# Single PSUM banks in place of half double banks in a hybrid encoder kernel

## The chip, the cores and the metric

The kernel runs on one core of one Trainium2 chip. The figure of merit is device microseconds of one execution. TensorE (PE) multiplies, VectorE (DVE), ScalarE (ACT) and GpSimd (POOL) do elementwise work, and SyncE (SP) issues the DMA transfers. Matmul results land in PSUM, which has 8 banks; one bank holds 512 float32 values in each of 128 partitions. A tile of 128 x 512 takes one bank, a tile of 128 x 1024 takes two neighbouring banks (a double bank).

## What is computed

Input and output are one sequence of 1024 tokens of width 1024 in float32. There are two layers, each a mixer and a squared-ReLU MLP, all residual with an RMSNorm ahead, and a final RMSNorm:

```python
for layer in range(DEPTH):                     # DEPTH = 2
    if layer % 2 == 0:
        h = rmsnorm(x, e_norm_mix[e])
        x = x + even_mixer(h, ...)             # windowed GQA + pooling mixer
    else:
        h = rmsnorm(x, o_norm_mix[o])
        x = x + odd_mixer(h, ...)              # latent attention + gated recurrence
    x = x + sq_relu_mlp(rmsnorm(x, norm_mlp[layer]), w_mlp1[layer], w_mlp2[layer])
return rmsnorm(x, final_norm)

def sq_relu_mlp(h, w1, w2):
    u = jax.nn.relu(h @ w1)                    # 1024 -> 4096
    return (u * u) @ w2                        # 4096 -> 1024
```

## The kernel before

The program runs through five stages: the even mixer (0 to about 310 us of the trace), the first MLP (to about 957), the odd mixer (to about 1493), the second MLP (to about 2097) and the final norm with the output. Activations are kept transposed, channels on the partitions and tokens on the free axis. A float32 operand is split into a high and a low part in the fast matmul format (L122 makes the high part on ACT, L130 the low part on DVE or POOL), and a product is three matmuls: high x high, high x low, low x high.

**The MLP.** The matrix product is done in 2 x 2 blocks of a seven-product scheme of the Strassen kind. The 4096 hidden channels are 16 pairs of blocks. One product is 12 matmuls of 128 x 512 into one bank of PSUM (L378 in the first matrix product, L498 in the second). A pair uses four banks a, b, c, d and makes seven products in the text's order a, b, c, d, then a, c and d once more: `head` puts the first product in a and copies it out (L396, ACT), `rest` makes the product b and adds it to that copy (L407, DVE), subtracts from c (L410), adds d (L412); then `head2` adds a second product into a, which is read by a ReLU on ACT (L401); c and d get a second product each, read at L419 and L424. The weight blocks are raw blocks or sums of raw blocks (made on POOL), split by L122 and L130 into the tiles `wb`.

**Where the banks come from.** Three pools hold PSUM: `pb` and `pa` with two single banks each, and `p2` with two double banks. In the MLP the pairs take turns (`banks`): the even ones take the four single banks, the odd ones the four halves of the two double banks. Elsewhere `PS` hands out places in turn for projections (`z`, `op`, `o`), sums of squares (`ss`) and broadcasts of the row norms (`rb`): two of `pb`, two of `pa`, and four halves of double banks (`PS2H`). In the attention parts `set_wide` leaves only the four single banks in the rotation, and the double banks hold scores (`s`, `ms`) and gates (`gt`).

**What a tile is.** Waits are made per tile. The two halves of a double bank are one tile, though they lie in two banks: a matmul into one half waits until earlier readers of the other half are done, and the double bank is free for the next user when both halves have been read. A framework orders the instructions of each engine ahead of the run, by operands and by free tiles, so the text's order is not the order on the engine; each engine then works through its own list strictly in turn.

**The norm between stages.** RMSNorm needs a sum over channels: squares are added on POOL or DVE (`square_add`, L245), a matmul with ones gives `ss` (L220), a chain of seven small DVE and ACT instructions makes `rr` (L196 to L211), a matmul against the identity broadcasts it as `rb` (L231), ACT copies it to `RB` (L235), and DVE scales the activations with it (L1528 ahead of an MLP).

Of the kernel before, what the change touches and what calls it, by code (L numbers as in the profile page):

```python
# [9 lines left out]
F32 = mybir.dt.float32  # L10
# [5 lines left out]
P = 128  # L16
S = 1024
# [7 lines left out]
N2 = 512  # L25
# [21 lines left out]
class Trunk:  # L47
    def __init__(self, tc, a, pools, phases):
        self.tc, self.nc, self.a = tc, tc.nc, a
        self.cst, self.gp, self.wp, self.tp, self.sm, self.pb, self.pa, self.p2, self.dr = pools  # L50
        nc = self.nc
        self.uid = 0
        self.cols = self.cst.tile([P, NCOLS], F32, tag="cols", name="cols")
        nc.sync.dma_start(self.cols, a["cols"])
        self.ident = self.cst.tile([P, P], F32, tag="ident", name="ident")
        make_identity(nc, self.ident)
        self.ones = self.cst.tile([P, 1], F32, tag="ones", name="ones")
        nc.vector.memset(self.ones, 1.0)
        self.wide = False
        self.pk = 0  # L60
        self.half = None
        self.halves = {}
        self.wreq = []
        self.wout = []
        for ph in phases:
            self.wreq += self.requests(ph)
# [19 lines left out]
    def PA(self, name):  # L86
        return self.pa.tile([P, N2], F32, tag="a", name=self.nm(name))

    def PS2(self, name):
        return self.p2.tile([P, S], F32, tag="bb", name=self.nm(name))  # L90

    def PS(self, name):

        k = self.pk
        self.pk = (k + 1) % (4 if self.wide else 8)
        return self.PB(name) if k < 2 else self.PA(name) if k < 4 else self.PS2H(name)

    def PS2H(self, name):

        if self.half is None:  # L100
            self.half = self.PS2(name)
            return self.half[:, :N2]
        h, self.half = self.half, None
        return h[:, N2:]

    def set_wide(self, w):
        self.wide = w
        self.pk = 0
        self.half = None

    def pin(self, ins):

# [170 lines left out]

    def banks(self, which):
        if which:
            two = [self.PS2("q"), self.PS2("q")]
            return [x[:, s] for x in two for s in (slice(0, N2), slice(N2, S))]
        return [self.PB("q"), self.PB("q"), self.PA("q"), self.PA("q")]

    def w_stream(self, l, order, second, look=0):  # L290
# [1396 lines left out]
def trunk(tc, a, phases=("even", "mlp0", "odd", "mlp1", "final")):  # L1687
    PSUM = bass.MemoryType.PSUM
    with tc.tile_pool(name="cst", bufs=1) as cst, tc.tile_pool(name="sm", bufs=4) as sm, \
            tc.tile_pool(name="tp", bufs=4) as tp, tc.tile_pool(name="wp", bufs=W_BUFS) as wp, \  # L1690
            tc.tile_pool(name="gp", bufs=G_BUFS) as gp, tc.tile_pool(name="pb", bufs=2, space=PSUM) as pb, \
            tc.tile_pool(name="pa", bufs=2, space=PSUM) as pa, \
            tc.tile_pool(name="p2", bufs=2, space=PSUM) as p2, \
            tc.tile_pool(name="dr", bufs=1, space=bass.MemoryType.DRAM) as dr:
        t = Trunk(tc, a, (cst, gp, wp, tp, sm, pb, pa, p2, dr), phases)
        gains = {"even": "e_norm", "odd": "o_norm", "mlp0": "mlp0", "mlp1": "mlp1"}
        xs = dr.tile([D, S], F32, tag="xs", name="xs")
        xm = [dr.tile([D, S], F32, tag=f"xm{i}", name=f"xm{i}") for i in range(2)]
        box = {}

        def follow(i):

            def make(X):
                ph = phases[i] if i < len(phases) else None
                box[i] = Out(t, X) if ph is None else Final(t, X) if ph == "final" else \
                    Norm(t, X, gains[ph], xs if ph == "odd" else None) if ph in ("even", "odd") else \
                    SNorm(t, X, gains[ph], xm[int(ph[-1])], int(ph[-1]))
                return box[i]
            return make

        X = [t.G("X") for _ in range(NC)]
        first = follow(0)(X)
        for cut in first.cuts:
            for c in range(NC):
                s = slice(*cut)
                tc.nc.sync.dma_start(X[c][:, s], a["x"][c * P:(c + 1) * P, s])
                first.part(c, cut)
        for i, ph in enumerate(phases):
            if ph == "even":
                X = t.even(box[i], follow(i + 1))  # L1720
            elif ph == "odd":
                X = t.odd(box[i], xs, follow(i + 1))
            elif ph != "final":
                t.mlp(int(ph[-1]), box[i], follow(i + 1), f"ut{ph[-1]}_")
# [87 lines left out]
```

## Time and profile before

| what | us |
|---|---|
| median of three runs | 2161.3 |
| the three runs | 2161.3, 2161.65, 2158.78 |
| the profiled execution's own time | 2161.66 |
| its span in the trace | 2159.5 |
| PE busy in the span | 2051.3 (95%) |
| DVE / ACT / POOL busy | 1542.9 / 1065.0 / 823.2 |

Rows of the trace's views read as "start, length, engine, operation out<-in, count"; in square brackets stands how long the engine idled before it and which instruction released it. L378 is line 378 of the kernel before. A matmul's listed length (some 0.39 us) is longer than its share of PE time, since matmuls follow each other in a pipeline. The profiled execution's time is 2.16 us over its span.

### The profile page before, as it was taken

Reading aid. Unit: us, or ns where it says so; the run is one execution under the profiler, and the core shown is the slowest. Engines: PE = TensorE matmul, PEld = TensorE weight load, DVE = VectorE, ACT = ScalarE, POOL = GpSimd, SP = SyncE. Lnnn points to the kernel's source line nnn. Section 1 sums busy time; section 2 is a strip of 40 time slices with the busy share of each in tenths; the row PEclk is TensorE's granted clock in tenths of the full one; section 3 lists DMA queues with packets and bytes.
Section 4 is the critical chain, followed back from the end, with each engine's and each line's share of the span. In section 5 each row is a group of like instructions: output and inputs, shape, how many; then the busy total and the mean of one; then the engine's idle time right before and its main releaser. Section 6 shows DMA issues by size and latency. Waiting matters only on the chain.

```text
span 2159.5 us, 27248 instructions
## 1 busy us (share of the span) xinstructions
PE 2051.3 (95%) x9600; PEld 1688.1 (78%) x9600; DVE 1542.9 (71%) x2365; ACT 1065.0 (49%) x1853; POOL 823.2 (38%) x635
## 2 busy tenths in 40 slices
PE   6989998999999999999997999999899999999997
PEld 5867776787777888888785898888678777788887
DVE  7688868765656877775898888717875655877964
ACT  5236645444544534340565777734645545544423
POOL 4133332332315142242557776463242321522414
PEclk9999999999999999999999999999999999999999
DMA  5630052543448535132102000245443445654302
GB/s 176 144 136 24 11 185 78 176 166 127 151 152 310 176 107 180 55 101 76 35 25 68 11 11 10 79 130 188 135 172 127 152 155 179 236 204 157 127 29 79
DMA packets 115544, 261.32 MB, mean 121 GB/s; under 512 B 19664, under 2 KB 21840, under 8 KB 115408
## 3 DMA queue, kind: packets, MB, share of 16 engines
q1 hardware_dynamic: 115408, 259.59, 35.7%
q8 instruction: 75, 1.23, 0.2%
q14 instruction: 61, 0.50, 0.1%
HBM read 178.28 MB, written 72.35 MB: 116 GB/s over the span
## 4 chain that ended last, share of the span: by engine, by line
PE 72%; DVE 12%; issue 5%; ACT 5%; DMA 3%; POOL 3%; SPq 0%; POOLq 0%; DVEq 0%; ACTq 0%
PE q L498 22%; PE q L378 22%; PE op L185 7%; PE z L185 6%; PE ms L1334 4%; PE o L185 3%; PE cav L1124 2%; PE ctp L1350 2%; DVE th L1443 1%; POOL acc L245 1%; DVE wb L130 1%; DMA X<-xm 1%; DMA raw<-in_e_w_in_dram 1%; PE tp L870 1%; DVE w L1433 0%
## 5 line engine op out<-in xcount | busy, mean ns | idle before, releaser
L378 PE MATMUL q<-hb,wb 128*128 128x512 f32 x2688 | 629.7, 394 | 34.6 <-DVE wb L130 9.8
L378 PEld LDWEIGHTS q<-hb,wb 128*128 128x128 f32 x2688 | 504.1, 189 | 158.2 <-DVE wb L130 12.8
L498 PE MATMUL q<-ub,wb 128*128 128x512 f32 x2352 | 539.3, 391 | 8.8 <-ACT wb L122 7.0
L498 PEld LDWEIGHTS q<-ub,wb 128*128 128x128 f32 x2352 | 443.2, 189 | 104.3 <-ACT wb L122 8.8
L130 DVE TENSOR_TENSOR wb<-raw,wb 128x512 fp32r<-128x512 f32 x268 | 226.6, 851 | 112.6 <-ACT wb L122 112.2
L122 ACT CAST wb<-raw 128x512 fp32r<-128x512 f32 x268 | 164.3, 619 | 183.0 <-PE q L378 112.7
L122 ACT CAST wb<-sum 128x512 fp32r<-128x512 f32 x152 | 93.8, 620 | 183.3 <-PE q L378 100.7
L130 DVE TENSOR_TENSOR ub<-ut,ub 128x512 fp32r<-128x512 f32 x168 | 136.3, 824 | 66.2 <-ACT ub L122 65.8
L122 ACT CAST ub<-ut 128x512 fp32r<-128x512 f32 x168 | 101.4, 618 | 147.2 <-DVE wb L130 18.8
L130 DVE TENSOR_TENSOR wb<-sum,wb 128x512 fp32r<-128x512 f32 x152 | 126.3, 833 | 22.5 <-ACT wb L122 21.5
L185 PE MATMUL z<-Hh,wh 128*128 128x512 f32 x328 | 129.8, 400 | 10.6 <-ACT wh L122 9.6
L245 POOL TENSOR_TENSOR acc<-acc,sq 128x512 f32<-128x512 f32 (+1 forms) x62 | 88.3, 1427 | 123.3 <-ACT sq L244 121.4
L185 PE MATMUL z<-Hl,wh 128*128 128x512 f32 x328 | 130.2, 397 | 4.1 <-DVE Hl L1471 4.0
L185 PE MATMUL z<-Hh,wl 128*128 128x512 f32 x328 | 129.1, 394 | 0.8 <-DVE wl L130 0.8
L323 POOL TENSOR_TENSOR sum<-raw,raw 128x512 f32<-128x512 f32 x28 | 40.3, 1448 | 215.6 <-DMA raw<-in_w_dram 184.4
L332 POOL TENSOR_TENSOR raw<-raw,raw 128x512 f32<-128x512 f32 x32 | 43.5, 1360 | 203.2 <-DVE wb L130 175.6
L1124 PE MATMUL cav<-cpT,VS 128*128 128x256 f32 x512 | 102.7, 305 | 3.6 <-ACT cpT L1353 2.3
L122 ACT CAST wh<-raw 128x1024 fp32r<-128x1024 f32 (+1 forms) x49 | 49.8, 1015 | 111.9 <-PE z L185 39.4
L1334 PE MATMUL ms<-Kt,Qt 128*128 128x512 f32 (+1 forms) x384 | 99.8, 396 | 2.2 <-ACT e L1341 1.4
L185 PE MATMUL op<-yh,wh 128*128 128x512 f32 x252 | 100.0, 398 | 1.4 <-DVE ya L887 0.9
L185 PE MATMUL op<-yl,wh 128*128 128x512 f32 x252 | 98.9, 393 | 0.0
L185 PE MATMUL op<-yh,wl 128*128 128x512 f32 x252 | 98.0, 393 | 0.0
(343 smaller groups left out, 3815.0 us busy)
## 6 DMA issues: line engine op xcount, KB each, us to landing
raw<-in_w_dram SPq DMA_DIRECT2D x140, 512.0 KB, 4.5
xm<-X SPq DMA_DIRECT2D x32, 256.0 KB, 2.0
X<-xm SPq DMA_DIRECT2D x16, 512.0 KB, 6.6
raw<-in_o_w_out_dram SPq DMA_DIRECT2D x16, 512.0 KB, 3.5
raw<-in_o_w_in_dram SPq DMA_DIRECT2D x11, 512.0 KB, 3.5
raw<-in_e_w_in_dram SPq DMA_DIRECT2D x10, 512.0 KB, 5.1
X<-in_x_dram SPq DMA_DIRECT2D x16, 256.0 KB, 5.6
raw<-in_e_w_out_dram SPq DMA_DIRECT2D x8, 512.0 KB, 3.6
```

What stands on the lines that cost most here:

```text
L122: self.nc.scalar.copy(out, x)
L130: e.tensor_tensor(out, x, y, op=ALU.subtract)
L185: self.nc.tensor.matmul(ps, l, r, start=(first and i == 0), stop=(last and i == n - 1))
L245: (eng or nc.gpsimd).tensor_tensor(acc, acc, sq, op=ALU.add)
L323: add(x, blk(p, 1, 0), blk(p, 1, 1), op=ALU.add)
L332: add(x, x, blk(p, 1, 0), op=ALU.add)
L378: nc.tensor.matmul(ps, a, b, start=(first and c == 0 and i == 0), stop=(c == 3 and i == 2), skip_group_check=True)
L498: nc.tensor.matmul(ps[m], a, b, start=(first and j == 0 and i == 0), stop=(j == len(pairs) - 1 and i == 2), skip_group_check=True)
L870: nc.tensor.transpose(tp[:, h * P:(h + 1) * P], pt[h // 2][:, o:o + P], self.ident)
L1124: nc.tensor.matmul(ACC[0][:, (p % 2) * 256:(p % 2 + 1) * 256], VS[h][:, kb * P:(kb + 1) * P], pp[:, t * N2 + ii * 256:t * N2 + (ii + 1) * ...
L1334: nc.tensor.matmul(ps[:, s], l[rows, qs], r[rows, s], start=(i == 0), stop=(i == 2))
L1350: nc.tensor.transpose(tp[:, (2 * i + j) * P:(2 * i + j + 1) * P], pr[j][:, kb * P:(kb + 1) * P], self.ident)
```

## The change

The double-bank pool `p2` stays for scores and gates. A new pool `pc` of four single banks stands beside it, and every product that took a half of a double bank takes a tile of `pc`: in `banks` for the odd pairs of the MLP, and in `PS` for the projections, sums and broadcasts. The pools now name 2 + 2 + 4 + 4 = 12 banks in all; the framework places their tiles in the 8 banks by the time at which each lives. The number of instructions on each engine, the operands and the transfers are the same; the line numbers move up by 7 or 8 (L378 becomes L370, L498 becomes L490, L185 becomes L178, L220 becomes L213, L231 becomes L224).

```diff
--- before.py
+++ after.py
@@ -47,7 +47,7 @@
 class Trunk:
     def __init__(self, tc, a, pools, phases):
         self.tc, self.nc, self.a = tc, tc.nc, a
-        self.cst, self.gp, self.wp, self.tp, self.sm, self.pb, self.pa, self.p2, self.dr = pools
+        self.cst, self.gp, self.wp, self.tp, self.sm, self.pb, self.pa, self.pc, self.p2, self.dr = pools
         nc = self.nc
         self.uid = 0
         self.cols = self.cst.tile([P, NCOLS], F32, tag="cols", name="cols")
@@ -58,7 +58,6 @@
         nc.vector.memset(self.ones, 1.0)
         self.wide = False
         self.pk = 0
-        self.half = None
         self.halves = {}
         self.wreq = []
         self.wout = []
@@ -86,6 +85,9 @@
     def PA(self, name):
         return self.pa.tile([P, N2], F32, tag="a", name=self.nm(name))
 
+    def PC(self, name):
+        return self.pc.tile([P, N2], F32, tag="c", name=self.nm(name))
+
     def PS2(self, name):
         return self.p2.tile([P, S], F32, tag="bb", name=self.nm(name))
 
@@ -93,20 +95,11 @@
 
         k = self.pk
         self.pk = (k + 1) % (4 if self.wide else 8)
-        return self.PB(name) if k < 2 else self.PA(name) if k < 4 else self.PS2H(name)
-
-    def PS2H(self, name):
-
-        if self.half is None:
-            self.half = self.PS2(name)
-            return self.half[:, :N2]
-        h, self.half = self.half, None
-        return h[:, N2:]
+        return self.PB(name) if k < 2 else self.PA(name) if k < 4 else self.PC(name)
 
     def set_wide(self, w):
         self.wide = w
         self.pk = 0
-        self.half = None
 
     def pin(self, ins):
 
@@ -283,8 +276,7 @@
 
     def banks(self, which):
         if which:
-            two = [self.PS2("q"), self.PS2("q")]
-            return [x[:, s] for x in two for s in (slice(0, N2), slice(N2, S))]
+            return [self.PC("q") for _ in range(4)]
         return [self.PB("q"), self.PB("q"), self.PA("q"), self.PA("q")]
 
     def w_stream(self, l, order, second, look=0):
@@ -1690,9 +1682,10 @@
             tc.tile_pool(name="tp", bufs=4) as tp, tc.tile_pool(name="wp", bufs=W_BUFS) as wp, \
             tc.tile_pool(name="gp", bufs=G_BUFS) as gp, tc.tile_pool(name="pb", bufs=2, space=PSUM) as pb, \
             tc.tile_pool(name="pa", bufs=2, space=PSUM) as pa, \
+            tc.tile_pool(name="pc", bufs=4, space=PSUM) as pc, \
             tc.tile_pool(name="p2", bufs=2, space=PSUM) as p2, \
             tc.tile_pool(name="dr", bufs=1, space=bass.MemoryType.DRAM) as dr:
-        t = Trunk(tc, a, (cst, gp, wp, tp, sm, pb, pa, p2, dr), phases)
+        t = Trunk(tc, a, (cst, gp, wp, tp, sm, pb, pa, pc, p2, dr), phases)
         gains = {"even": "e_norm", "odd": "o_norm", "mlp0": "mlp0", "mlp1": "mlp1"}
         xs = dr.tile([D, S], F32, tag="xs", name="xs")
         xm = [dr.tile([D, S], F32, tag=f"xm{i}", name=f"xm{i}") for i in range(2)]
```

The order in which the framework puts the instructions moves with it. Three places on PE follow; `x3` are three matmuls that read alike, and buffer numbers differ between the two programs.

**In the steady first matrix product of an MLP, PE, a pair that took double banks.** Before, `q_4164` holds products a and b, `q_4165` products c and d; the rows are the last of c, then b, then the second product of a, then d:

```order
L378 MATMUL q_4165<-hb_3168,wb_4093 128x512 x3
L378 MATMUL q_4164<-hb_3034,wb_4072 128x512 x3
L378 MATMUL q_4164<-hb_3060,wb_4072 128x512 x3
L378 MATMUL q_4164<-hb_3086,wb_4072 128x512 x3
L378 MATMUL q_4164<-hb_3112,wb_4072 128x512 x3
L378 MATMUL q_4164<-hb_2913,wb_4132 128x512 x3
L378 MATMUL q_4164<-hb_2935,wb_4132 128x512 x3
L378 MATMUL q_4164<-hb_2957,wb_4132 128x512 x3
L378 MATMUL q_4164<-hb_2961,wb_4132 128x512 x3
L378 MATMUL q_4165<-hb_3192,wb_4112 128x512 x3
L378 MATMUL q_4165<-hb_3195,wb_4112 128x512 x3
L378 MATMUL q_4165<-hb_3198,wb_4112 128x512 x3
```

With the change a, b, c, d are `q_4185` to `q_4188`; the rows are the last of b, then c, d and the start of the second product of a:

```order
L370 MATMUL q_4186<-hb_3126,wb_4093 128x512 x3
L370 MATMUL q_4187<-hb_3152,wb_4114 128x512 x3
L370 MATMUL q_4187<-hb_3156,wb_4114 128x512 x3
L370 MATMUL q_4187<-hb_3179,wb_4114 128x512 x3
L370 MATMUL q_4187<-hb_3183,wb_4114 128x512 x3
L370 MATMUL q_4188<-hb_3207,wb_4133 128x512 x3
L370 MATMUL q_4188<-hb_3210,wb_4133 128x512 x3
L370 MATMUL q_4188<-hb_3213,wb_4133 128x512 x3
L370 MATMUL q_4188<-hb_3216,wb_4133 128x512 x3
L370 MATMUL q_4185<-hb_2926,wb_4153 128x512 x3
L370 MATMUL q_4185<-hb_2948,wb_4153 128x512 x3
L370 MATMUL q_4185<-hb_2970,wb_4153 128x512 x3
```

The second product of a stood right behind b, in the same tile; now 24 matmuls of c and d stand between, and a and b are two tiles.

**At the start of the even mixer, PE.** `Hh` and `Hl` are the parts of the loaded input's eight channel blocks, and `z_341` is one double bank that holds a projection in each half, from weights `wh_214` and `wh_220`. Before, behind the last block of the first projection, the whole second one follows:

```order
L185 MATMUL z_276<-Hh_158,wl_221 128x512
L220 MATMUL ss_301<-ones,acc_107 128x1 x4
L185 MATMUL z_341<-Hh_158,wh_214 128x512
L185 MATMUL z_341<-Hl_159,wh_214 128x512
L185 MATMUL z_341<-Hh_158,wl_215 128x512
L185 MATMUL z_341<-Hh_103,wh_220 128x512
L185 MATMUL z_341<-Hl_104,wh_220 128x512
L185 MATMUL z_341<-Hh_103,wl_221 128x512
L185 MATMUL z_341<-Hh_110,wh_220 128x512
```

The 24 matmuls of the second projection (`z_341<-..,wh_220` and its `wl_221`) end with the broadcast `rb_318` one row ahead of the last. With the change the two projections are `z_344` and `z_369`, and both go along with each block as it comes:

```order
L178 MATMUL z_279<-Hl_162,wh_223 128x512
L178 MATMUL z_279<-Hh_161,wl_224 128x512
L213 MATMUL ss_304<-ones,acc_110 128x1 x4
L178 MATMUL z_344<-Hh_161,wh_217 128x512
L178 MATMUL z_369<-Hh_161,wh_223 128x512
L178 MATMUL z_344<-Hl_162,wh_217 128x512
L178 MATMUL z_344<-Hh_161,wl_218 128x512
L178 MATMUL z_369<-Hl_162,wh_223 128x512
L178 MATMUL z_369<-Hh_161,wl_224 128x512
L224 MATMUL rb_321<-ident,rr_319 128x128 x4
L178 MATMUL z_472<-Hh_106,wh_229 128x512
```

The broadcast `rb_321` now follows the last block at once.

**At the start of the first MLP, PE.** The sum and the broadcast of the second half of the tokens. Before:

```order
L378 MATMUL q_3063<-hb_2842,wb_2884 128x512 x3
L378 MATMUL q_3063<-hb_2888,wb_2884 128x512 x3
L378 MATMUL q_3063<-hb_2892,wb_2884 128x512 x3
L220 MATMUL ss_2989<-ones,acc_2758 128x1 x4
L378 MATMUL q_3171<-hb_2838,wb_3037 128x512 x3
L378 MATMUL q_3171<-hb_2842,wb_3037 128x512 x3
L378 MATMUL q_3171<-hb_2888,wb_3037 128x512 x3
L378 MATMUL q_3171<-hb_2892,wb_3037 128x512 x3
L231 MATMUL q_3006<-ident,rr_3004 128x128 x4
L378 MATMUL q_3006<-hb_2913,wb_2966 128x512 x3
```

With the change:

```order
L370 MATMUL q_2977<-hb_2948,wb_2893 128x512 x3
L370 MATMUL q_2977<-hb_2970,wb_2893 128x512 x3
L370 MATMUL q_2977<-hb_2974,wb_2893 128x512 x3
L213 MATMUL ss_3002<-ones,acc_2769 128x1 x4
L370 MATMUL q_3019<-hb_2926,wb_2979 128x512 x3
L370 MATMUL q_3019<-hb_2948,wb_2979 128x512 x3
L370 MATMUL q_3019<-hb_2970,wb_2979 128x512 x3
L370 MATMUL q_3019<-hb_2974,wb_2979 128x512 x3
L224 MATMUL rb_3037<-ident,rr_3017 128x128 x4
L370 MATMUL q_3077<-hb_2850,wb_2896 128x512 x3
```

The broadcast was a half of the tile `q_3006`, and the product `q_3171` with `wb_3037` stood ahead of it; now it has the tile `rb_3037`, and a product with another weight block (`wb_2979`) stands ahead of it. Further up the list the output projections `op` of the even mixer now all stand ahead of the MLP's first product; before, two matmuls of it stood among them.

## The prediction

> **What bounds the kernel now.** I read the page's busy times first, then its chain of work that ended last, then the table by stage, then the list of PE's waits.
>
> ```profile
> span 2159.5 us, 27248 instructions
> PE 2051.3 (95%) x9600; PEld 1688.1 (78%) x9600; DVE 1542.9 (71%) x2365; ACT 1065.0 (49%) x1853; POOL 823.2 (38%) x635
> PE 72%; DVE 12%; issue 5%; ACT 5%; DMA 3%; POOL 3%; SPq 0%; POOLq 0%; DVEq 0%; ACTq 0%
> ```
>
> PE is busy for 2051.3 of 2159.5 us, so whatever a better use of the banks can bring lies within 108 us of PE idling, less what the first loads and the last norm need. No matmul is removed. The next view is busy time by stage; its columns are the window, its length, then busy time and instructions of PE, PE's weight loads, DVE, ACT and POOL, then PE's granted clock, the DMA share and GB/s.
>
> ```profile
> 0.00:62.00 62.00, 45.49 (x185) 35.03 (x186) 42.15 (x76) 30.65 (x47) 29.12 (x26) 0.94 0.45 153
> 62.00:121.00 59.00, 59.00 (x264) 48.84 (x263) 37.23 (x59) 12.35 (x19) 7.35 (x5) 1.00 0.64 152
> 310.00:405.00 95.00, 81.89 (x335) 64.20 (x334) 80.08 (x118) 49.77 (x90) 29.34 (x17) 0.95 0.38 134
> 405.00:645.00 240.00, 234.29 (x1018) 189.65 (x1017) 142.50 (x200) 117.49 (x194) 67.33 (x49) 1.00 0.44 153
> 645.00:697.00 52.00, 47.78 (x198) 37.76 (x198) 33.38 (x37) 25.24 (x45) 29.55 (x20) 0.97 0.82 296
> 697.00:924.00 227.00, 226.97 (x1001) 188.00 (x1002) 179.14 (x249) 96.59 (x165) 62.06 (x40) 1.00 0.39 132
> 957.00:1493.00 536.00, 510.65 (x2733) 433.04 (x2732) 400.25 (x557) 309.22 (x494) 307.41 (x238) 0.98 0.22 67
> 1575.00:1817.00 242.00, 235.38 (x1020) 189.82 (x1018) 144.07 (x200) 116.65 (x193) 67.80 (x49) 1.00 0.43 151
> 1817.00:1870.00 53.00, 47.83 (x200) 38.48 (x201) 36.87 (x38) 26.24 (x47) 31.30 (x20) 0.97 0.88 317
> ```
>
> The second matrix product (697 to 924) has PE at 226.97 of 227: nothing to win. The first matrix product of each MLP (405 to 645, 1575 to 1817) idles 5.7 and 6.6 us while DVE and ACT are far from full. The starts (0 to 62, 310 to 405) idle 16.5 and 13.1 us. The passages to the second product (645 to 697, 1817 to 1870) idle 4 to 5 us at a DMA share of 0.82 and 0.88. A matmul takes 227/1001 = 0.227 us of PE. Which waits make the idling, by the list of PE's waits (total us, times, longest):
>
> ```profile
> PE q L378 <- DVE wb L130: 9.8, 6, 3.4
> PE q L498 <- ACT wb L122: 7.0, 4, 2.6
> PE q L378 <- DVE t L407: 7.0, 9, 0.8
> PE q L378 <- DVE u L410: 6.8, 8, 1.4
> PE q L378 <- ACT t L396: 4.2, 4, 2.0
> PE q L378 <- DVE u L412: 1.7, 2, 0.9
> PE q L378 <- ACT RB L235: 0.7, 1, 0.7
> ```
>
> The first two are weights that came late; a bank has no part in them. The other five are releases of PSUM: 7.0 + 6.8 + 4.2 + 1.7 + 0.7 = 20.4 us, 24 times. Some of them are true dependences (the same product's bank is read, then written), some come only from two products sharing a tile. The chain of waits and PE's timeline tell these apart in the steady part:
>
> ```profile
> 474.74 3.56 PE L378 MATMUL q<-hb,wb 128*128 128x512 f32 x15
> 479.09 39.00 PE L378 MATMUL q<-hb,wb 128*128 128x512 f32 x168 [0.79 <-DVE t L407]
> 518.87 26.34 PE L378 MATMUL q<-hb,wb 128*128 128x512 f32 x113 [0.78 <-DVE t L407]
> ```
>
> Each batch of 168 matmuls is two pairs (2 x 7 x 12); once in two pairs PE stops for L407. L407 reads product b; the matmul that waits writes the second product of a. They are two banks but one tile, on the pair that takes double banks. The pair in single banks has the same order of work and no stop.
>
> **The change part by part.** (1) *Steady first product.* By the new order the second product of a stands 24 matmuls (24 x 0.227 = 5.4 us) behind b, and in another tile, so the L407 waits (7.0) go whole, with the L412 (1.7) and L396 (4.2) ones of the shared tiles. Of the eight L410 waits some are a true dependence, c read before c is written again:
>
> ```profile
> 373.66 13.88 PE L378 MATMUL q<-hb,wb 128*128 128x512 f32 x60 [0.50 <-DVE u L410]
> 403.96 14.33 PE L378 MATMUL q<-hb,wb 128*128 128x512 f32 x62 [1.41 <-DVE u L410]
> ```
>
> The second MLP repeats both (8 waits, two such pairs of 0.50 and 1.41), so 3.8 of the 6.8 us may stay. That leaves 20.4 - 3.8 = 16.6, less the RB wait (0.7, priced below): about 16. The second matmul sets take over at once, if their weights are ahead: in the two quoted batches no matmul waits for one. A new stop of the same kind stands at one place in each MLP, where the new order has c's two products back to back, some 0.5 us each. I take 15 us; bounds 10 (weights come late behind a third of them) and 19 (each wait has also some 0.15 us of issue around it, 479.09 - 474.74 - 15 x 0.227 = 0.94 against 0.79).
>
> (2) *Start of the even mixer.* PE's rows around the last input block, and behind it:
>
> ```profile
> 35.50 0.39 PE L185 MATMUL z<-Hh,wh 128*128 128x512 f32 x1
> 40.72 1.05 PE L231 MATMUL rb<-ident,rr 128*128 128x128 f32 x8
> 44.62 1.87 PE L220 MATMUL ss<-ones,acc 128*128 128x1 f32 x8 [2.61 <-POOL acc L245]
> 46.92 0.63 PE L185 MATMUL z<-Hl,wh 128*128 128x512 f32 x1
> 51.17 0.40 PE L185 MATMUL z<-Hh,wl 128*128 128x512 f32 x1
> 54.15 0.49 PE L625 MATMUL vtp<-ident,vt 128*128 128x128 f32 x3
> 38.83 0.16 DVE L211 TENSOR_TENSOR rr<-r,t 128x4 f32<-128x4 f32 x1
> ```
>
> The 24 matmuls of the second half of the double bank run from 35.50 to 41.5, when everything is loaded, although PE had idled between the blocks. In the new order they go with the blocks. The broadcast may then start when rr is ready (39.0) and the next projection behind it, near 41, where it now ends at 54.15 after the 2.61 us stop and a stretch of matmuls 0.43 us apart (46.92 to 51.17, ten of them) instead of 0.227. At best that projection ends 54.15 - (41 + 5.4) = 7.7 us sooner. But the next sum still waits for POOL's squares (44.5), and POOL gets the two products with RB (1.26 us each) ahead of its last squares, so the second broadcast comes at some 52 to 53 instead of 55.17. I take 5, bounds 2 and 7. From 62 to 121 PE is at 59.00 of 59, so an earlier PE carries it on.
>
> (3) *Start of the first MLP.*
>
> ```profile
> 328.97 0.74 PE L378 MATMUL q<-hb,wb 128*128 128x512 f32 x2
> 330.69 4.14 PE L378 MATMUL q<-hb,wb 128*128 128x512 f32 x10 [0.98 <-DVE wb L130]
> 334.67 1.05 PE L231 MATMUL q<-ident,rr 128*128 128x128 f32 x8
> 336.39 3.02 PE L378 MATMUL q<-hb,wb 128*128 128x512 f32 x12 [0.68 <-ACT RB L235]
> 332.22 0.16 DVE L211 TENSOR_TENSOR rr<-r,t 128x4 f32<-128x4 f32 x1
> 336.37 5.39 DVE L1528 SCALAR_TENSOR_TENSOR X<-X,cols,RB 128x512 f32<-128x512 f32 x8
> ```
>
> rr is there at 332.38, the broadcast starts at 334.67 behind a product that waited for its weight, and DVE starts on the second half at 336.37. DVE is what sets the pace here (80.08 of 95). In the new order the sum stands 16 matmuls earlier (3.6 us), and the broadcast follows it after 12. I take 4, bounds 0 (the other weight block is late too) and 6. The second MLP's start has no such row, 0 to 1, taken as part of (1).
>
> (4) *The end.* One stop of PE in the last projection is a shared tile, and the last sum comes 1 us later by it:
>
> ```profile
> 2143.05 0.39 PE L185 MATMUL o<-Uh,wh 128*128 128x256 f32 x1 [0.52 <-DVE X L561]
> ```
>
> I take 1, bounds 0 and 1.5.
>
> (5) *The passages to the second product.* The same order on PE as far as it matters. PE arrives up to 16 us earlier (5 + 4 + half of 15), and the weights, transfers and POOL sums must arrive earlier too. They are released by buffers that PE frees:
>
> ```profile
> 475.62 0.62 ACT L122 CAST wb<-raw 128x512 fp32r<-128x512 f32 x1 [1.61 <-PE q L378]
> 674.99 4.60 PE L498 MATMUL q<-ub,wb 128*128 128x512 f32 x12 [2.64 <-ACT wb L122]
> ```
>
> The cast of a weight waited for PE, so mostly the stream moves along; but where DMA is at 0.82 to 0.88 for 50 us it can't be pushed faster. I take 2 us given back, bounds 0 and 8.
>
> (6) The odd mixer uses only `pb`, `pa` and double banks in its loops: nothing, under 1 us either way. The second matrix product: nothing.
>
> Sum: 15 + 5 + 4 + 1 - 2 = 23 us. 2161.7 (this execution's own time, 0.4 over the median of 2161.3) - 23 = **2138.7 us**.
>
> The Trainium skill, "Perfetto Trace Analysis", Optimizing Tensor Performance, Matmuls, says independent matmul groups should rotate through different PSUM banks so that the reading of one overlaps the next. By its letter the kernel before already does (eight banks in turn), and (1) would be 0; the 0.79 us row at 479.09 shows that the wait goes by tile here, not by bank.
>
> **Rivals.** *Given back.* The stops of (1) go, but starts and passages are held by DVE, POOL and DMA: (2) 2, (3) 0, (4) 0, (1) 15, (5) -7: 10 us, 2151.7. For it: DVE at 80.08 of 95, the 3.4 us weight wait, DMA at 0.88. Against: between the passages PE is full, and a lead can't be lost there.
>
> *No change.* Each stop removed comes back as a wait for the next weight block, since the splits are paced by something else; the starts stay. 2161.7 to within 4. For it: the 9.8 and 7.0 us of weight waits lead the list. Against: batches of 168 matmuls without one. [...]
>
> *Slower.* In the new order c and d of every pair are written again 24 matmuls (5.4 us) after their first product, in place of being spaced unevenly. If ACT's and DVE's lists put weight splits ahead of the reads L410 and L412, so that a read is later than 5.4 us behind its product, every pair stops, not every second. Price by the row at 479.09: 32 pairs x 0.94 = 30 us against the 15 gained: 2161.7 + 30 - 15 = 2177. It decides from about half a us per pair on (32 x 0.5 = 16). Against it: now a read follows its product within 1 to 2 us. That the change doesn't do what it says is out: the new order shows each product in its own tile.
>
> **Chances.** Forecast (2128 to 2147) 0.60; given back (2147 to 2157) 0.24; no change 0.09; slower 0.07. A measurement here can tell 0.2% (4.3 us) from no change: faster 0.84, same 0.09, slower 0.07. The lower bound is all the upper gains, 19 + 7 + 6 + 1.5 = 33.5: 2128. The upper one is 10 + 2 - 8 = 4 saved: 2157. The forecast's own range is 2128 to 2147.
>
> **What would show it.** In the waits of PE the rows of L407, L412 and most of L396 and L410 are gone (under 4 us together); in the timeline the batches of 168 have no stop between them and the first products take 234 and 235 us instead of 240 and 242. The broadcast at the start comes right behind the last load; at the first MLP it follows rr within 1 us. Wrong would be: the idle time of L378 now under weights (L130, L122), stops each pair, or passages over 60 us long.

## The result, and the profile after

The changed kernel takes 2134.7 us (median of four runs, 2130.21 to 2139.7) against 2161.3 before: a ratio of 0.9885, 95% interval 0.9872 to 0.9898, so 26.6 us faster. The forecast was 2138.7, range 2128 to 2157. The profiled execution took 2131.94 us with a span of 2130.2, 29.3 less than the profiled span before.

The page of the changed kernel, its busy times and the chain by engine:

```profile
span 2130.2 us, 27341 instructions
PE 2035.0 (96%) x9600; PEld 1687.7 (79%) x9600; DVE 1548.0 (73%) x2365; ACT 1069.0 (50%) x1853; POOL 826.7 (39%) x635
PE 77%; DVE 9%; issue 4%; ACT 4%; DMA 3%; POOL 2%; SPq 0%; POOLq 0%; ACTq 0%; DVEq 0%
```

PE's idle time fell from 108.2 to 95.2 us, only 13 of the 29 us. The other 16 are "busy" time that the same 9600 records no longer take, some 8 of them in the two loops (the steady first products of the MLPs). What is left of the stops shows in the list of PE's waits (total us, times, longest), and where the time went in the table by stage (window, length, then PE's busy time and matmuls, and so on as before):

```profile
PE q L490 <- ACT wb L115: 9.9, 5, 3.0
PE q L370 <- DVE u L402: 9.2, 7, 2.5
PE q L370 <- ACT t L388: 6.5, 4, 2.9
PE q L370 <- DVE wb L123: 5.0, 3, 2.7
```

```profile
0.00:62.00 62.00, 48.93 (x215) 39.05 (x216) 44.94 (x77) 31.62 (x49) 29.74 (x26) 1.00 0.45 153
300.00:396.00 96.00, 81.88 (x333) 64.84 (x332) 81.14 (x116) 49.88 (x90) 28.20 (x16) 0.93 0.39 141
396.00:627.50 231.50, 231.27 (x1020) 191.27 (x1020) 147.52 (x200) 117.22 (x192) 69.89 (x49) 1.00 0.44 155
627.50:679.50 52.00, 47.56 (x201) 38.26 (x199) 32.86 (x37) 26.39 (x47) 29.48 (x20) 0.97 0.92 323
1556.00:1787.00 231.00, 231.00 (x1019) 191.32 (x1020) 146.67 (x200) 117.33 (x192) 69.25 (x49) 1.00 0.45 158
```

The L399 group (L407 before) is gone, and so are the L404 one (L412 before) and the wait of `q` for RB; L402 (L410 before) has grown from 6.8 to 9.2 us and L388 (L396) from 4.2 to 6.5. The two loops are full: 231.27 of 231.50 us, where the same 1020 matmuls took 241 and 243 us before. PE's timeline shows it in two rows; the second is one batch of 922 matmuls, 209.28 us or 0.227 each, that ran through eleven pairs:

```profile
395.74 27.94 PE L370 MATMUL q<-hb,wb 128*128 128x512 f32 x122 [1.49 <-DVE u L402]
423.91 209.28 PE L370 MATMUL q<-hb,wb 128*128 128x512 f32 x922 [0.23 <-DVE u L402]
```

Both programs issue 9488 matmuls on PE (the page's 9600 has two records for each of the 112 in the norms' sums and broadcasts), so the k-th one of each can be compared. The lead of the changed kernel at the same k, and how much of it each stretch brought:

| stretch (times of the trace before) | forecast | changed kernel | a second execution of it |
|---|---|---|---|
| start of the even mixer, to 166 | 5 (2 to 7) | 9.2 | 4.9 |
| rest of the even mixer, to 311 | 0 | 1.4 | 1.4 |
| start of the first MLP, to 398 | 4 (0 to 6) | -2.3 | -0.7 |
| its loop, to 659 | about 7 | 9.1 | 9.2 |
| passage and second product, to 938 | -1 | 0.3 | -1.0 |
| odd mixer, to 1502 | 0 | -0.5 | -2.2 |
| start of the second MLP, to 1583 | 0 to 1 | 1.5 | 1.6 |
| its loop, to 1821 | about 8 | 11.9 | 11.6 |
| passage, to 1874 | -1 | -1.4 | -0.2 |
| the end | 1 | 0.1 | 0.1 |
| sum | 23 | 29.2 | 24.7 |

The 1.4 us of the rest of the even mixer were forecast at nothing. Matched in the same way, every profile below with single banks in the rotation has 1.4 or 1.5 there, every one with double banks 0.0 or 0.1.

### The profile page after: what moved, and what is told of

Read it like the earlier page. It is cut to its first block, busy times and chain, and to the rows that moved or that the text cites. A ratio compares the mean times of both kernels' runs of the same rounds, so it can differ in the third digit from the quotient of the medians.

```text
span 2130.2 us, 27341 instructions
## 1 busy us (share of the span) xinstructions
PE 2035.0 (96%) x9600; PEld 1687.7 (79%) x9600; DVE 1548.0 (73%) x2365; ACT 1069.0 (50%) x1853; POOL 826.7 (39%) x635
## 4 chain that ended last, share of the span: by engine, by line
PE 77%; DVE 9%; issue 4%; ACT 4%; DMA 3%; POOL 2%; SPq 0%; POOLq 0%; ACTq 0%; DVEq 0%
PE q L370 25%; PE q L490 21%; PE op L178 8%; PE z L178 7%; PE ms L1326 4%; PE o L178 3%; PE cav L1116 2%; PE ctp L1342 2%; DMA raw<-in_w_dram 1%; DVE th L1435 1%; DVE wb L123 1%; PE tp L862 1%; PE av L870 1%; PE gt L178 1%; DMA raw<-in_e_w_in_dram 1%
## 5 line engine op out<-in xcount | busy, mean ns | idle before, releaser
L370 PE MATMUL q<-hb,wb 128*128 128x512 f32 x2688 | 622.3, 393 | 20.8 <-DVE u L402 9.2
L370 PEld LDWEIGHTS q<-hb,wb 128*128 128x128 f32 x2688 | 508.7, 190 | 132.5 <-ACT t L388 8.2
L490 PE MATMUL q<-ub,wb 128*128 128x512 f32 x2352 | 537.8, 391 | 11.1 <-ACT wb L115 9.9
L490 PEld LDWEIGHTS q<-ub,wb 128*128 128x128 f32 x2352 | 442.2, 188 | 106.5 <-ACT wb L115 12.0
L178 PE MATMUL z<-Hh,wh 128*128 128x512 f32 x336 | 130.9, 397 | 10.4 <-ACT wh L115 9.7
L178 PE MATMUL z<-Hl,wh 128*128 128x512 f32 x336 | 132.5, 394 | 1.2 <-DVE Hl L1463 1.2
L178 PE MATMUL z<-Hh,wl 128*128 128x512 f32 x336 | 131.5, 392 | 0.7 <-DVE wl L123 0.7
L319 POOL TENSOR_TENSOR sum<-raw 128x512 f32<-128x512 f32 x32 | 47.8, 1494 | 182.0 <-DVE T L424 69.8
L178 PE MATMUL op<-yh,wh 128*128 128x512 f32 x256 | 100.8, 395 | 1.2 <-DVE ya L879 0.8
L178 PE MATMUL op<-yl,wh 128*128 128x512 f32 x256 | 99.6, 390 | 0.0
L178 PE MATMUL op<-yh,wl 128*128 128x512 f32 x256 | 99.6, 390 | 0.0
```

The lines of the kernel that those rows point to most:

```text
L178: self.nc.tensor.matmul(ps, l, r, start=(first and i == 0), stop=(last and i == n - 1))
L319: add(s1, blk(p, 1, 0), blk(p, 1, 1), op=ALU.add)
L370: nc.tensor.matmul(ps, a, b, start=(first and c == 0 and i == 0), stop=(c == 3 and i == 2), skip_group_check=True)
L490: nc.tensor.matmul(ps[m], a, b, start=(first and j == 0 and i == 0), stop=(j == len(pairs) - 1 and i == 2), skip_group_check=True)
```

## The experiments

**Where the spread between executions lies.** Its own runs differ by 9 us, so the changed kernel ran again, unedited.

> The changed kernel once more, without an edit, to see where its runs of 2130 to 2140 us differ. If the spread lies in what waits for transfers (the first loads, the two passages to the second matrix product), a slower execution shows longer stops there and the same matmul times between; if it lies in the clock, long runs of matmuls without a wait take more than 0.2267 us each.

2136.5 us (2136.43 to 2138.46), ratio 0.9899 (0.9883 to 0.9916). The last column above is its profile. The first expectation holds for 1.3 us in the first passage only (in the second this execution is 1.2 us better); the second does not hold for long runs, since the full loops agree to 0.3 us. What differs most is the matmuls behind stops. The mean granted clocks are 0.983 and 0.987. In the table by stage, the same stretch (130 to 160 us, the pooling part) of this execution, and then of the changed kernel's first profile:

```profile
130.00:160.00 30.00, 26.20 (x99) 19.88 (x98) 24.70 (x64) 17.33 (x39) 13.05 (x11) 0.77 0.45 176
```

```profile
130.00:160.00 30.00, 25.48 (x116) 19.01 (x114) 27.25 (x77) 20.44 (x46) 15.31 (x15) 0.94 0.45 176
```

At a granted clock of 0.77 instead of 0.94, PE did 99 matmuls in more busy time than the other's 116; it came 1.35 us later to this stretch and left the mixer's start 4.3 us behind. Counting matmuls of 512 columns that follow their predecessor by 0.40 to 0.46 us instead of 0.227, the two executions have 94 and 71. That is 23 x 0.2 = 4.6 us, the size of the difference between them (24.7 against 29.2). Stretch by stretch the two do not go together throughout: up to 166 us this execution has 15 more slow ones, 3.0 of its 4.3 us, but in the second passage it has 13 more and is 1.2 us better. So slow matmuls are a part of the spread, and the rest stays open. The Trainium skill's "TensorE: Matmul & The Clock Gate", Part 1, has the clock fall after an idle window and the windows run free of the kernel, so that the number of slow matmuls varies from run to run. The two counts agree with that; no run here shows the window itself.

**Half of the change.** The rotation gets the single banks of `pc`; `banks` stays as in the kernel before. (Against the kernel before; the lines that add the pool are left out.)

```diff
-        return self.PB(name) if k < 2 else self.PA(name) if k < 4 else self.PS2H(name)
+        return self.PB(name) if k < 2 else self.PA(name) if k < 4 else self.PC(name)
 ...
     def banks(self, which):
         if which:
             two = [self.PS2("q"), self.PS2("q")]
```

> Half of the change: the rotation for projections, sums and broadcasts takes single banks, the odd MLP pairs keep the halves of two double banks. Tile theory: the gain of the two loops (some 21 us between the checkpoints of the two traces) stays out, that of the even mixer's start (9 us up to the pooling part) is there, 2149 to 2156 us, and the stops at the second product of a are back, once in two pairs. Rival (the loops gain because of what the start delivers earlier): the loops gain too, under 2145. Rival (only the loops count): 2158 to 2162.

2153.3 us, ratio 0.9974 (0.9964 to 0.9983): in the tile theory's range. The loops keep all their stops (timeline of this run):

```profile
476.36 38.91 PE L381 MATMUL q<-hb,wb 128*128 128x512 f32 x168 [0.79 <-DVE t L410]
516.06 29.23 PE L381 MATMUL q<-hb,wb 128*128 128x512 f32 x126 [0.79 <-DVE t L410]
```

By matched matmuls the loops gained 0.2 and 1.1 us, against 9.1 and 11.9. One thing was not as expected: at the 200th matmul the start had brought 1.5 us, where the two executions of the changed kernel have 6.9 and 5.5 (2.6 against 9.2 and 4.9 at 166 us), although PE's list over the first 240 rows is the same as the changed kernel's. The rows of this run, and of the changed kernel, show where:

```profile
39.19 1.13 PE L234 MATMUL rb<-ident,rr 128*128 128x128 f32 x8 [1.79 <-DVE rr L214]
44.12 0.79 PE L188 MATMUL z<-Hh,wh 128*128 128x512 f32 x1 [3.80 <-DVE vt L600]
```

```profile
39.01 1.16 PE L224 MATMUL rb<-ident,rr 128*128 128x128 f32 x8 [1.46 <-DVE rr L204]
40.84 0.50 PE L178 MATMUL z<-Hh,wh 128*128 128x512 f32 x1 [0.67 <-ACT RB L228]
```

By what released it, the projection behind the broadcast was placed in another bank. In the changed kernel it took the broadcast's own bank, free after a 0.58 us copy on ACT; here the bank of an earlier projection that DVE reads at L600. DVE's rows show why that read is late:

```profile
38.97 4.50 DVE L133 TENSOR_TENSOR wl<-raw,wh 128x1024 fp32r<-128x1024 f32 x2
43.39 0.68 DVE L600 TENSOR_TENSOR vt<-z,RB 128x512 f32<-128x512 f32 x1
```

The norm had been copied by 40.95 (on ACT from 40.36 on, 0.59 us), but two weight splits of 4.50 us stood ahead of the read in DVE's list. 3.80 us of waiting against 0.67, with the same instructions in the same order on PE: the gain at the start hung on the bank in which a tile was laid, and on what the reader of that bank did first.

**Double banks, paired otherwise.** If sharing a tile is what costs, double banks need not go; they need other partners.

```diff
-            return [x[:, s] for x in two for s in (slice(0, N2), slice(N2, S))]
+            return [x[:, s] for s in (slice(0, N2), slice(N2, S)) for x in two]
```

> The kernel before with one index order changed: products a and c share one double bank and b and d the other, instead of a with b and c with d. Nothing else is edited and no single banks are added. Tile theory: now no product stands right behind the one that it shares a tile with, so the L407 stops go and the two loops gain what the change gained there, some 19 to 21 us, with the starts as before: 2139 to 2146 us. Rival (a bank of its own is what counts): a double bank is as slow as ever, 2158 to 2165.

2143.25 us (2142.12 to 2145.64), ratio 0.9929 (0.9914 to 0.9944), inside the tile theory's range. No wait for L407 or L412 is left in PE's list. One row of its timeline, which the window ends, holds 441 matmuls without a stop, over five pairs, in halves of double banks:

```profile
459.64 100.70 PE L378 MATMUL q<-hb,wb 128*128 128x512 f32 x441
```

From 398 to 659 us of the trace before it gained 8.5 us, from 1583 to 1821 11.5. So one index order, and nothing else, gives nearly the loops' whole gain; the rival that a bank of its own counts falls.

**The third pairing.** a with d, b with c.

```diff
-            two = [self.PS2("q"), self.PS2("q")]
-            return [x[:, s] for x in two for s in (slice(0, N2), slice(N2, S))]
+            x, y = self.PS2("q"), self.PS2("q")
+            return [x[:, :N2], y[:, :N2], y[:, N2:], x[:, N2:]]
```

> The kernel before with the third way to pair: a and d share one double bank, b and c the other. Tile theory: c's second product now stands only 2 matmuls behind its first one on PE in the odd pairs, because the other products are held off by their tile partners, so PE stops once in two pairs for L410's read, some 0.9 to 1.3 us each as at 388.71 in the trace before; the loops gain nothing: 2157 to 2166 us. Rival (any pairing that parts a from b gains): 2139 to 2146 as with a and c, b and d.

2201.4 us, ratio 1.0189 (1.0171 to 1.0208): 40 us slower, and my number was a miss of 35. The rival falls, but the theory had the wrong place: it put the stops into the loops. The loss is in the first six pairs of each MLP (waits of PE, then timeline):

```profile
PE q L378 <- DVE u L410: 30.9, 12, 4.7
```

```profile
407.08 13.67 PE L378 MATMUL q<-hb,wb 128*128 128x512 f32 x48 [4.73 <-DVE u L410]
423.76 16.17 PE L378 MATMUL q<-hb,wb 128*128 128x512 f32 x70 [1.50 <-DVE u L410]
444.05 13.98 PE L378 MATMUL q<-hb,wb 128*128 128x512 f32 x48 [4.12 <-DVE u L410]
```

In those pairs the first product lies in a tile of the rotation and `rest` gets the first three of the four places as b, c and d. So c and d shared a tile, and d waited for L410's read of c. Two runs split it.

```diff
-    def banks(self, which):
+    def banks(self, which, first=False):
         if which:
+            x, y = self.PS2("q"), self.PS2("q")
+            if first:
+                return [x[:, :N2], y[:, :N2], y[:, N2:], x[:, N2:]]
+            return [x[:, :N2], x[:, N2:], y[:, :N2], y[:, N2:]]
 ...
-            bk = self.banks(k)
+            bk = self.banks(k, True)
```

> The kernel before, where only the first six pairs of each MLP are paired as in the run with a and d, b and c together. In these pairs the first product lies elsewhere and the four places go to b, c and d, so it is c and d that share a tile in every second of them; the later pairs stay as they were. Theory: the 40 us which that run lost come from d waiting for L410's read of c, which is late while DVE still has the start's work: 2185 to 2205 us. Rival (the later pairs lost them): 2157 to 2165.

> The other part: the first six pairs as before, only the later ones with a and d, b and c together. Theory: one stop in two pairs takes the place of the L407 stop (0.71 us idle against 0.79), so the loops gain at most 3 us: 2155 to 2163. Rival (parting a from b is what gains): 2140 to 2150.

(The second has `if not first`.) 2197.4 us, ratio 1.0176 (1.0158 to 1.0194), and 2162.5 us, ratio 1.0013 (1.0004 to 1.0023), each in the range of its theory. The parts add up: +38 and +3 against +40. In the first, the L410 read (L412 here) again heads the waits:

```profile
PE q L380 <- DVE u L412: 29.2, 10, 4.7
```

These stops come to 22 us more than before, and 43 more slow matmuls follow stops (127 against 84, some 8.6 us). In the second the stop in the loops has only changed its releaser (PE, then ACT):

```profile
478.41 38.93 PE L380 MATMUL q<-hb,wb 128*128 128x512 f32 x168 [0.71 <-ACT wb L122]
477.74 0.62 ACT L122 CAST wb<-raw 128x512 fp32r<-128x512 f32 x1 [2.05 <-PE q L380]
```

The same two double banks thus give 2143, 2160, 2162, 2197 or 2201 us by who shares a tile with whom. That the stop waits for a weight and not for a read was not foreseen for the third pairing, whose trace showed it first. The cast of that weight itself waited 2.05 us for PE, until the batch ahead ended at 477.71: it seems to need a buffer that PE frees too late in this order. No run isolates why; this stays open.

**The start of the MLPs.** Here the changed kernel lost 2.3 us (0.7 in the second execution) where a gain of 4 was forecast. Its rows at the broadcast on PE, then the last step of `rr` and the work behind the broadcast on DVE, then the first complete pairs on PE:

```profile
317.97 1.29 PE L213 MATMUL ss<-ones,acc 128*128 128x1 f32 x8 [1.52 <-DVE acc L238]
319.12 4.33 PE L370 MATMUL q<-hb,wb 128*128 128x512 f32 x12
323.29 1.05 PE L224 MATMUL rb<-ident,rr 128*128 128x128 f32 x8
320.54 0.17 DVE L204 TENSOR_TENSOR rr<-r,t 128x4 f32<-128x4 f32 x1
325.11 5.39 DVE L1520 SCALAR_TENSOR_TENSOR X<-X,cols,RB 128x512 f32<-128x512 f32 x8 [0.28 <-ACT RB L228]
362.38 13.85 PE L370 MATMUL q<-hb,wb 128*128 128x512 f32 x60 [1.41 <-DVE u L402]
378.78 15.48 PE L370 MATMUL q<-hb,wb 128*128 128x512 f32 x60 [2.55 <-DVE u L402]
```

DVE's scaling starts 336.37 - 325.11 = 11.26 us earlier than before, but PE came to the MLP 10.6 us earlier already: the broadcast itself brought 0.7. It stood behind 12 matmuls that took 4.33 us, 0.36 each, behind two stops, and the sum ahead had waited for squares; `rr` had been there since 320.71. From there DVE needs 37 us up to the first pair in both kernels. Then PE stops for L402 longer than before (2.55 against 1.17 us at the second pair), in this execution with eight slow matmuls behind the stop (15.48 against 13.85 us for 60). Two edits of the changed kernel: the first holds one product behind the broadcast.

```diff
-            product(ps, nb.T["B21"], False, True)
+            product(ps, nb.T["B21"], False, True, hold=(p == 1))
 ...
+                    if hold and c == 0 and i == 0:
+                        self.pin(m)
```

> The changed kernel with one matmul product at each MLP's start held behind the row norm's broadcast, so that the broadcast directly follows the sum of squares on PE. Theory (DVE's list behind that broadcast sets the pace of the MLP's start): the copy of the broadcast comes some 2.6 us earlier relative to the sum, DVE's block of work behind it too, and the first MLP's loop begins 1 to 3 us earlier; over both MLPs 2 to 5 us less than the changed kernel. Rival (late weights or POOL sums set the pace): no difference, under 1 us.

2122.3 us (2122.17 to 2122.53), ratio 0.9831 (0.9816 to 0.9845): 14 us under the changed kernel's 2136.5 on the same chip, with 2 to 5 expected.

```profile
320.70 2.08 PE L224 MATMUL rb<-ident,rr 128*128 128x128 f32 x8 [1.50 <-DVE rr L204]
361.60 27.45 PE L370 MATMUL q<-hb,wb 128*128 128x512 f32 x120 [0.88 <-DVE u L404]
```

The broadcast starts 2.6 us earlier at the same entry, and the stop between the two batches of 60 is gone: one batch of 120. Against the second profile of the changed kernel, the two MLP starts bring 2.8 + 0.7 = 3.5 and 5.5 - 1.6 = 3.9 us; the other 7 us lie in the mixers, which the edit does not touch; this execution had 51 slow matmuls in all against 94, 8.6 us by 0.2 each. Against the first profile the two starts bring 2.8 + 2.3 = 5.1 and 5.5 - 1.5 = 4.0, nearly all of the 9.8 us between the two spans. The direction is the theory's. The starts' own 7 to 9 us go beyond its 2 to 5; the stop that went and the slow matmuls are candidates, which no run separates. Whether the 7 us in the mixers are chance stays open too: four runs of each lie at 2122.2 to 2122.5 and at 2136.4 to 2138.5.

The second edit moves the four differences of a finished pair behind the next pair's first reads.

```diff
-            V.tensor_tensor(x1, u12, u11, op=ALU.subtract)
-            put(p, "T1", x1)
 ...
+            def combos():
+                V.tensor_tensor(x1, u12, u11, op=ALU.subtract)
+                put(p, "T1", x1)
 ...
+            due.append(combos)
```

with `while due: due.pop()()` in the next pair behind L404 and its ReLU.

> The changed kernel, where the four differences of a finished pair (L422 to L428, for the second matrix product) are written behind the next pair's first reads of PSUM instead of ahead of them. Theory (at the start of each MLP the read of c is late because DVE's list has these differences ahead of it): the stops for L402 at the first pairs (1.41, 2.55, 1.49 and 0.88, 1.32, 1.39 us idle in the trace of the changed kernel, and slow matmuls behind them) shrink by half or more, 3 to 7 us less than the changed kernel: 2129 to 2133. Rival (weights and POOL hold these pairs): within 1 us of the changed kernel, 2135 to 2138.

2124.7 us (2121.09 to 2128.36), ratio 0.9834 (0.9814 to 0.9853): 10 to 12 us under the changed kernel by times, 11 to 14 by ratios (0.9834 against 0.9885 and 0.9899), with 3 to 7 expected. By matched matmuls the MLPs' starts and loops brought 29.7 us, against 20.2 and 21.6 in the changed kernel's two executions. The stops behind the first pair are gone; from there 231 matmuls run through:

```profile
367.77 52.61 PE L370 MATMUL q<-hb,wb 128*128 128x512 f32 x231 [1.12 <-DVE u L403]
```

So DVE's list did hold the reads back: PE waited for L402 because DVE worked off L422 to L428 first. In the changed kernel's trace the last of them and the read that released PE at 378.78 follow each other:

```profile
376.21 1.63 DVE L428 TENSOR_TENSOR T<-u,T 128x512 f32<-128x512 f32 x1
377.94 0.69 DVE L402 TENSOR_TENSOR u<-q,t 128x512 f32<-128x512 f32 x1
```

Then both edits together.

> Both edits, the broadcast ahead of one product at each MLP's start and the four differences later. If they mend different waits, the gains add: 14 us and e6's. If the broadcast's order had already ordered the first pairs (its trace shows one batch of 120 matmuls there in place of two of 60), little is left for the second: 2119 to 2123.

2118.5 us (2116.62 to 2120.45), ratio 0.9805 (0.9790 to 0.9820), half a us under the range set for the case that little is left for the second edit: the two overlap for the most part. It is the fastest of all, 42 us under the kernel before. Its timeline at the first MLP:

```profile
363.93 56.24 PE L370 MATMUL q<-hb,wb 128*128 128x512 f32 x247 [0.88 <-DVE u L405]
```

## Why the prediction was right, and which of its steps were not

The time came within 4 us of the forecast and the mechanism was the one named: waits go by tile, and the products that had stood in one tile no longer stop each other. The pairing runs show this; single banks are one way to it. That the sum came so close is in part luck: the loops brought 6 us more than their term, and the start of the first MLP 5 to 6 us less than its.

*Step (1), the loops: right in mechanism, too small.* 21 us (9.1 + 11.9), above my 15 and its upper bound of 19. The clock has no part in it: it is 1.00 in the loops' rows by stage before and after, and neither kernel has a slow matmul there. The term went wrong in two ways that partly cancel. First, most of the L396 and L410 rows that I counted do not lie in the loops. PE's waits in the first loop before (405 to 645) are these:

```profile
PE q L378 <- DVE t L407: 3.1, 4, 0.8
PE q L378 <- DVE wb L130: 1.0, 1, 1.0
PE q L378 <- DVE u L412: 0.9, 1, 0.9
PE q L378 <- DVE u L410: 0.3, 1, 0.3
```

The 4.2 us of L396 stand at the two MLPs' starts; they did not go with the shared tiles but became 6.5. Second, the term was sized by idle rows of 0.79 to 0.94 us per stop. From start to start, the two quoted batches before lie 518.87 - 479.09 = 39.78 us apart for 168 matmuls, which at 0.2267 are 38.08: 1.70 us lost in two pairs. The idle row leaves out the last matmul's end, the slower first step behind the stop (0.11 us more) and the short second stop for the copy of L396. Four such double pairs are 6.8 of the first loop's 9.1 us. The weight waits in the two loops (1.0 and 1.9 us), which I had left in place, went too.

*Step (2), the start of the even mixer: 9.2 and 4.9 us in two executions, 2.6 in a kernel with the same list on PE there.* The forecast of 5 with bounds 2 and 7 is not confirmed as a property of the change. The new order of projections and broadcast was there as read, but what decided between these was the bank of the next projection, which I had not looked at, and in part how long PE ran slowly.

*Step (3), the start of the first MLP: wrong.* It had the sum 3.6 us earlier and the broadcast 12 matmuls behind it at full speed. The sum waited 1.52 us for squares, and the 12 matmuls took 4.33 us, so that the broadcast came 2.6 us behind `rr` and not within 1. And it did not follow the L402 waits to the first pairs: "3.8 of the 6.8 us may stay" became 9.2.

*Steps (4), (5), (6).* The end brought 0.1, not 1: the stop of 0.52 us went, and the sum behind it waited 1.54 us for DVE in place of 0.80. The passages gave back -0.3 to 1.0 and 0.2 to 1.4 us, where 2 were set in all; the first one's DMA share of 0.82, which I took for a limit, rose to 0.92. The odd mixer lost 0.5 and 2.2.

*Rivals.* "Given back" had the same term for the loops, and the first MLP's start nearer than I; it missed because the even mixer's start did pay and the passages took less than its 7. "No change" falls by the batch of 922: the weights kept up with an uninterrupted PE. "Slower" falls by the same row; a late read does stop PE, though, as the 9.2 us of L402 at the first pairs show, and 38 us with c and d in one tile.

*What would show it:* L407 and L412 gone, held. "Under 4 us together" for what is left of L396 and L410 failed, 15.7. The loops took 231 us, under the 234 forecast.

## What to carry to other kernels

Where a framework makes waits per tile, a tile over two PSUM banks makes two results wait for each other that need not: look at which product stands right behind its partner's reader, since pairing alone moved this kernel between 2143 and 2201 us. Price a PE stop from start to start of long batches, not by its idle row, and allow for slow matmuls behind a long one. When a stop is gone, follow the in-order list of the engine that reads PSUM: 10 us of the next gain here lay in what DVE did ahead of those reads.

## What the hardware showed that I had not expected

The same stop, at the same place and of the same length, is followed by slow matmuls in one execution of a program and by none in another. In the second execution of the changed kernel the row of the second pair reads:

```profile
383.10 13.86 PE L370 MATMUL q<-hb,wb 128*128 128x512 f32 x60 [2.55 <-DVE u L402]
```

In the first it took 15.48 us, with eight matmuls 0.43 us apart. Behind the L402 stops of 1.1 to 1.5 us neither execution has a slow one (13.85 us for 60); behind the 4.12 and 4.73 us stops of the third pairing there are 7 to 13. So the length of a stop does not decide alone, and how many slow matmuls a program has differs between its executions: 94 and 71, at mean granted clocks of 0.983 and 0.987. The 4.5 us between those two profiles are the size of some gains sought here, so single profiles of a start are not enough to price an edit there.
